# Two-layer hybrid diffusion step on one core: another order at the end of the expert stage and around the out-projection

## The chip, the cores and the metric

The kernel runs on one core of a Trainium2 chip. The metric is the device time of one execution in microseconds (us), as a median of several runs. Five engines work side by side, each through its own instructions in a fixed order: TensorE (PE, matrix products), VectorE (DVE), ScalarE (ACT), GpSimd (POOL) and SyncE (SP), which issues most of the transfers. An instruction that has to wait holds up everything behind it on its engine.

## What is computed

The reference runs two layers over 128 context tokens and 512 latent tokens of width 1024. Cut to what matters here:

```python
for l in range(DEPTH):                       # DEPTH = 2
    h = modulated(x)                         # scale and shift from the conditioning
    qa, ka, va, qb, kb, vb, qc, kc, vc, gc = split(h @ w_in)
    A = windowed attention(rope(qa), rope(ka), va, cached keys, sink)
    B = neighbourhood attention(qb, kb, vb, relative bias)
    C = swish(gc) * groupnorm(retention(qc, kc, vc, states))
    x = layernorm(alpha * x + gate * (concat(A, B, C) @ w_out))
    p = softmax(modulated(x) @ w_router)     # 16 experts, each takes its best tokens
    for e in range(16):                      # 64 latent and 16 context tokens each
        y[e] = (silu(xe @ w_gate) * (xe @ w_up)) @ w_down
    x = layernorm(alpha * x + gate * scatter(p * y))
```

All matrices are float32; the kernel splits each operand of a projection in a high part and a low part and multiplies three times (`mm3`: high by high, high by low, low by high).

## The kernel before

The 640 tokens are five tiles of 128: tiles 0 to 3 hold latent tokens, tile 4 the context. In each layer the work goes through four stages: the projections with the three head groups, the out-projection with the router, the experts, and the end of the experts with the second LayerNorm. Most of the order on the engines comes from a scheduler that works with the order in which the program is written, with `tc.issue_after(x)` (do not stand ahead of x) and with pools of buffers of limited size.

**Splitting.** `split` (L340 on) makes the high part on ACT (L344) and the low part on DVE or, with `E=G`, on GpSimd (L345). `weights(...)` does so for a chunk of weights of 1 MB: `wh` is the high part, `wl` the low part.

**Out-projection** (L1495 to L1545). For each tile `t`, `retention(u, cs)` (L1207 on) is started for the tiles `u` up to `t + 1`, one ahead. It makes scores (L1221), the products L1239 and L1243 into a PSUM buffer of the group "A", and then a chain of small instructions on one `work` buffer: the mean, L1252 (DVE), L1253 (ACT), L1255, L1256 and the root (DVE, then GpSimd L392), L1259, L1260 (DVE). After it PE transposes the result (L691, two matmuls) and a split puts it into `cs`, the operand of the tile's product. The product itself is L348 to L350, on PSUM buffers of group "A" too, in two halves of 512 columns with the weights `wo[0]`, `wo[1]` and then `wo[2]`, `wo[3]`; `wo[1]` and `wo[3]` are split on GpSimd (`WO = "0101"`). After the first half come L1373, L1374 (DVE), which write the residual tile `z`, the transposes L1387 and the logits L1395 of the router, which read a copy by ACT (L1391) or DVE (L1402).

**Experts** (L1873 to L1910). Per expert eight chunks `w_gate_up` (L1723, L1727) and four chunks `w_down` of 1 MB each go through 25 slots (`N_SLOTS`), loaded by SP. `down(e, aT)` (L1775) multiplies chunk by chunk: per chunk first the latent part (`lat`), then the context part (`cxt`). A slot comes free after its chunk.

**End of the experts.** Experts 0 to 13 are added to the token table in memory; the last two stay on chip. `on_chip` (L1810 on) weights the result of expert 14 (i = 0) and 15 (i = 1) and splits it: latent rows at L1819 and L1826, context rows at L1829, L1831, L1834. `begin` and `combine` (L1930, L1932) add them through one-hot matrices to the five tiles in PSUM. `ln2` (L1960 on) then walks a list, `OR1` between the layers and `OR2` after the last. Its steps are C (combine), L (statistics L610 to L616 and norm L1991), H (`turn_tile`: transposes L628, then the split into `hhi` and `hlo`, the operands of the next layer's projection), S (`store`: GpSimd L2011, L2014 over 128 x 1024, then the transfer to `xres`, L2015) and T (`tile_A`: the first projection of the next layer, keys and values of group A). `first_w` (L706) is the weight chunk of that first projection; its low part is made on DVE by four instructions of 128 x 512. `HG` (L117) says for which tile the half `kk = 0` of the `hlo` split is on GpSimd. After T4 follow the rotary step `rope` (L698 on: DVE L701, GpSimd L702, DVE L703 and L704) for the keys and then for each block of queries, and the chunks ci = 0, 1, ... of the next projection, each with a `wh` and a `wl`.

Of the kernel before, what the change touches and what calls it, by code (L numbers as in the profile page):

```python
# [63 lines left out]
OR1 = ["C0", "C1", "L0", "H0", "C2", "L1", "H1", "S0", "C3", "L2", "H2", "T0", "S1", "C4", "L3", "H3", "T1", "S2", "L4", "H4", "T2", "T3", "S3", "T4", "S4"]  # L64
OR2 = ["C0", "C1", "L0", "C2", "L1", "C3", "L2", "C4", "L3", "L4"]
# [12 lines left out]
NR = 1  # L78
# [32 lines left out]
NB = 0  # L111
# [4 lines left out]
SG = "0"  # L116
HG = "10000"  # L117
# [125 lines left out]
def hybrid_backbone_kernel(ctx: ExitStack, tc: tile.TileContext, a: dict):  # L243
# [94 lines left out]
    lo_op, hi_op = [], []  # L338

    def split(hi, lo, src, parts=1, E=V):  # L340
        w = src.shape[-1] // parts
        for i in range(parts):
            s = (Ellipsis, slice(w * i, w * i + w)) if parts > 1 else (Ellipsis,)
            hi_op[:] = [S.activation(hi[s], src[s], AF.Copy)]  # L344
            lo_op[:] = [E.tensor_tensor(lo[s], src[s], f32(hi[s]), op=ALU.subtract)]  # L345

# [362 lines left out]
    def start_A(l, w=None, first_in=False):  # L709
# [10 lines left out]
        ck = work()  # L720
        ld(ck[:, 0:128], a["cak"][l])
        split(kAh[:, 384:512], kAl[:, 384:512], ck[:, 0:128])
# [24 lines left out]
        return {"tab": tab, "kA": kA, "va": va}, tile_A  # L747

    def mixer(l, h, A, bg):
# [456 lines left out]

        def retention(t, cs):  # L1207
# [52 lines left out]
            V.tensor_mul(dd[:, 0:256], dd[:, 0:256], gC[:, 256 * t:256 * t + 256])  # L1260
# [227 lines left out]
        for t in range(NT):  # L1488
            ret = iter(())
            for u in range(t + 2):  # L1490
                if u == NT or u < NR or u in started:
                    continue
                started.add(u)
                if u < 4:
                    css[u] = sl.get(F32R, "cs")  # L1495
                ret = retention(u, css[u])
                if u == t:
                    drain(ret)
                else:
                    next(ret)  # L1500
# [36 lines left out]
        wo += [weights(AH_P, KP, E=G if WO[2 + i] == "1" else V) for i in range(2)]  # L1537
# [65 lines left out]
    def moe(l, gsel, idx, early, GB1, init, ctx_places, picked):  # L1603
# [171 lines left out]
        def down(e, aT):  # L1775
            last = e - (NE - 2)
            pl, pc = (psA(), psA()) if last == 1 else (psB(), psB())
            for k in range(4):
                ahead.fill(99, keep(e))
                w = ahead.next()  # L1780
                with in_turn("T"):
                    for i in range(2):
                        lat(pl, aT, w[:, 1024 * i:1024 * i + 1024], 2 * k + i)
                    for i, n in ((0, 0), (0, 1), (1, 0), (1, 1)):
                        cxt(pc, 2 * i + n, aT, w[:, 1024 * i + 512 * n:1024 * i + 512 * n + 512], 2 * k + i, k == 0, k == 3)
                sl.free(w)
# [22 lines left out]
        def on_chip(i, e, pl, pc, y):  # L1809
# [7 lines left out]
            for n in range(2):  # L1817
# [3 lines left out]
                with tc.issue_after((lo_op[0] if i and l + 1 < DEPTH else sq_last[0]).ins):  # L1821
# [6 lines left out]
            tC, yc = hf.get(F32, "yC"), hf.get(F32, "yc")  # L1828
            S.activation(tC[0:64, 0:512], pc[64:128], AF.Copy)  # L1829
            with tc.issue_after(lo.ins):  # L1830
                V.tensor_tensor(tC[0:64, 512:1024], pc[0:64], tC[0:64, 0:512], op=ALU.add)  # L1831
                for n in range(2):
                    r = slice(32 * n, 32 * n + 32)
                    V.scalar_tensor_tensor(yc[q, 512 * n:512 * n + 512], tC[r, 512:1024], gateC[r, e:e + 1],  # L1834
                                           g2[r, 512:1024], op0=ALU.mult, op1=ALU.mult)
                split(Ch[q], Cl[q], yc[q])
            hf.free(tC, yc)
# [75 lines left out]
        hf.free(aTs, last_aT, g2)  # L1913
# [38 lines left out]

        begin(0)
        begin(1)
        return combine, sums.ins

    def ln2(l, combine, sums):
# [44 lines left out]
        def store(t):  # L2002
# [6 lines left out]
            if SPN:  # L2009
                with tc.issue_after(pool_last[0]):  # L2010
# [7 lines left out]
        for f, t in [(o[0], int(o[1])) for o in (OR2 if h is None else OR1)]:  # L2018
            if f == "C":
                xs.append(combine(t))  # L2020
            elif f == "L":
                norm(t)
            elif f == "H":
# [171 lines left out]
```

## Time and profile before

| | us |
|---|---|
| median of 3 runs (lowest to highest) | 1911.55 (1911.55 to 1911.81) |
| the profiled execution | 1910.83 |
| its span on the trace | 1909.1 |
| PE busy | 1804.8 (95%) |
| DVE busy | 1137.1 (60%) |
| ACT busy | 423.9 (22%) |
| POOL busy | 242.0 (13%) |

The span goes from the first to the last instruction; 1.7 us of the profiled execution lie around it. Layer 0's out-projection lies at about 325 to 415 us of the span, its experts at 434 to 943, the boundary between the layers at 943 to 1020; layer 1's out-projection lies at about 1253 to 1344, its experts at 1365 to 1873, and the end of the last layer at 1873 to 1909. A busy share of 95% for PE says little about a place: what counts there is the gap ahead of an instruction on PE and the engine that ended it.

### The profile page before, as it was taken

What the parts mean: (1) busy time and instruction counts of PE and PEld (TensorE: products, weight loads), DVE (VectorE), ACT (ScalarE), POOL (GpSimd) and SP (SyncE); (2) the same over time, 40 slices, a digit from 0 to 9 for tenths busy, and PEclk for the clock granted to TensorE, in tenths of its full rate; (3) what the DMA queues carried; (4) which work ended last, traced back from release to release, by engine and by line L of the source; (5) the groups of instructions that cost most, each with busy time, mean ns of one, the idle gap of its engine ahead of it and who ended that gap; (6) DMA issues with size and microseconds to landing.
All of it is one profiled execution on the core that took longest, in us unless ns stands there. A gap on an engine that the chain in (4) does not pass through costs nothing.

```text
span 1909.1 us, 34582 instructions
## 1 busy us (share of the span) xinstructions
PE 1804.8 (95%) x14223; PEld 901.1 (47%) x14223; DVE 1137.1 (60%) x2968; ACT 423.9 (22%) x898; POOL 242.0 (13%) x188
## 2 busy tenths in 40 slices
PE   6999999899999999999879999998899999999995
PEld 3866777773333332222257767787533333222222
DVE  3654537566565655475586555574685757465657
ACT  2354533221000000000153655322200000000002
POOL 3200002221100000000061000121300000000003
PEclk9999999998999999999989999998899999999998
DMA  9333544289999999999933343325999999999994
GB/s 375 117 134 138 200 152 134 108 322 347 397 398 397 397 398 400 401 408 415 400 115 131 127 141 135 107 83 209 345 399 400 399 397 399 398 398 407 408 416 165
DMA packets 95886, 554.62 MB, mean 291 GB/s; under 512 B 13818, under 2 KB 18832, under 8 KB 36336
## 3 DMA queue, kind: packets, MB, share of 16 engines
q1 hardware_dynamic: 89776, 532.71, 70.7%
q0 software_dynamic: 5952, 19.69, 4.3%
q8 instruction: 112, 1.84, 0.4%
q14 instruction: 46, 0.38, 0.1%
HBM read 526.31 MB, written 26.05 MB: 289 GB/s over the span
## 4 chain that ended last, share of the span: by engine, by line
PE 56%; DMA 35%; DVE 5%; issue 2%; ACT 1%; POOL 0%; SPq 0%; DVEq 0%; ACTq 0%; POOLq 0%
DMA w<-wgu 22%; DMA w<-wdn 10%; PE pA L1723 10%; PE pA L348 7%; PE pA L349 6%; PE pA L350 6%; PE pA L1727 5%; PE pB L1723 3%; PE pB L356 2%; PE pC L813 2%; PE pB L1727 2%; PE pA L517 2%; PE pA L917 1%; PE pB L1395 1%; PE pA L1485 1%
## 5 line engine op out<-in xcount | busy, mean ns | idle before, releaser
L1723 PE MATMUL pA<-w,xT 128*32 128x512 f32 x4096 | 488.3, 597 | 12.0 <-DMA w<-wgu 9.3
L1723 PEld LDWEIGHTS pA<-w,xT 128*32 128x32 f32 x4096 | 130.0, 110 | 326.3 <-issue 275.7
L1727 PE MATMUL pA<-w,xT 128*32 128x512 f32 x2048 | 263.8, 592 | 0.0
L1723 PE MATMUL pB<-w,g 128*32 128x512 f32 x1920 | 229.8, 596 | 7.1 <-DMA w<-wdn 7.1
L1727 PEld LDWEIGHTS pA<-w,xT 128*32 128x32 f32 x2048 | 66.2, 110 | 153.6 <-issue 153.0
L1723 PEld LDWEIGHTS pB<-w,g 128*32 128x32 f32 x1920 | 61.2, 110 | 154.9 <-issue 122.4
L1727 PE MATMUL pB<-w,g 128*32 128x512 f32 x960 | 124.8, 592 | 0.0
L1642 DVE STREAM_TRANSPOSE g<-z 32x128 f32<-32x128 f32 x384 | 116.2, 303 | 6.4
L1642 DVE STREAM_TRANSPOSE catB<-xg 32x256 f32<-32x256 f32 x240 | 104.4, 435 | 4.0
L348 PE MATMUL pA<-hhi,wh 128*128 128x512 f32 x224 | 92.0, 411 | 0.0
L350 PE MATMUL pA<-hhi,wl 128*128 128x512 f32 x224 | 88.2, 396 | 0.6 <-DVE wl L328 0.6
L349 PE MATMUL pA<-hlo,wh 128*128 128x512 f32 x224 | 88.2, 394 | 0.0
L1805 POOL DMA_INDIRECT acc<-catB,idx x22 | 31.3, 1424 | 437.6 <-DVE catB L1801 437.6
L1765 ACT ACTIVATE z<-pA 128x512 f32<-128x512 f32 x18 | 10.7, 597 | 336.8 <-DVE xT L1659 165.6
L1642 DVE STREAM_TRANSPOSE g<-xg 32x128 f32<-32x128 f32 x240 | 72.6, 303 | 3.9
L345 DVE TENSOR_TENSOR wl<-w,wh 128x1024 fp32r<-128x1024 f32 (+2 forms) x46 | 54.5, 1220 | 33.4 <-ACT wh L344 13.9
L1623 POOL DMA_INDIRECT xg<-znd,idx x30 | 35.1, 1171 | 293.4 <-DVE catB L1642 238.6
L348 PE MATMUL pA<-wh,cs 128*128 128x512 f32 x160 | 68.0, 426 | 0.5 <-DVE gC L1140 0.3
L344 ACT ACTIVATE wh<-w 128x1024 fp32r<-128x1024 f32 (+2 forms) x50 | 53.7, 1119 | 61.9 <-DMA w<-win 25.0
L1727 PEld LDWEIGHTS pB<-w,g 128*32 128x32 f32 x960 | 31.1, 110 | 72.6 <-issue 72.6
L348 PE MATMUL pA<-wh,hhi 128*128 128x256 f32 x192 | 59.5, 313 | 5.7 <-ACT hhi L344 3.8
L350 PE MATMUL pA<-wh,cs 128*128 128x512 f32 x160 | 64.5, 405 | 0.0
(530 smaller groups left out, 2918.7 us busy)
## 6 DMA issues: line engine op xcount, KB each, us to landing
w<-wgu SPq DMA_DIRECT2D x256, 1024.0 KB, 21.5
w<-wdn SPq DMA_DIRECT2D x128, 1024.0 KB, 21.3
wada<-wada SPq DMA_DIRECT2D x48, 1024.0 KB, 4.9
w<-win SPq DMA_DIRECT2D x20, 1024.0 KB, 7.1
w<-wout SPq DMA_DIRECT2D x8, 1024.0 KB, 5.2
znd<-z SPq DMA_DIRECT2D x8, 512.0 KB, 5.7
acc<-z SPq DMA_DIRECT2D x8, 512.0 KB, 14.8
bias<-bias SPq DMA_DIRECT2D x8, 384.0 KB, 4.8
```

Source lines behind the costliest of these rows:

```text
L344: hi_op[:] = [S.activation(hi[s], src[s], AF.Copy)]
L345: lo_op[:] = [E.tensor_tensor(lo[s], src[s], f32(hi[s]), op=ALU.subtract)]
L348: T.matmul(out, lh, rh, start=first, stop=False)
L349: T.matmul(out, lh, rl, start=False, stop=False)
L350: return T.matmul(out, ll, rh, start=False, stop=last).ins
L356: T.matmul(out, (lh, ll)[x], (rh, rl)[y], start=first, stop=last)
L517: T.matmul(pm[32 * g:32 * g + 32, :], mst[:, k, :], w[:, 512 * g:512 * g + 512], start=(k == 0), stop=(k == 7))
L813: T.transpose(pt[:, 128 * b:128 * b + 128], s[:, o + 128 * b:o + 128 * b + 128], ident)
L1623: r = G.indirect_dma_start(out=xg[0:CAP, 0:1024], out_offset=None, in_=znd[l], in_offset=IndirectOffsetOnAxis(ap=idx[:, e:e + 1], axis=0))
L1642: sq_last[:] = [V.transpose(out, rows.rearrange("p (k q f) -> p k q f", q=4, f=32)[:, :, q, :])]
L1723: last_of["T"] = T.matmul(p[32 * g:32 * g + 32], x[:, 64 * ko + 32 * i:64 * ko + 32 * i + 32], w[:, 512 * n:512 * n + 512], start=(ko == 0 ...
L1727: last_of["T"] = T.matmul(p[32 * g:32 * g + 32], x[:, 512 + 32 * ko:544 + 32 * ko], w, start=first, stop=last).ins
```

## The change

1. `NR` goes from 1 to 2 and the loop of the out-projection runs to `t + 3`: retention is started two tiles ahead of the tile whose product is written. `wo[2]` is split on DVE in two parts, not ahead of the last retention's L1260; `wo[3]` is split on GpSimd as before.
2. In `OR1` the stores S0 to S4 move behind T2 and later, and are not to stand ahead of the last split on GpSimd (`g_op`).
3. The context part of expert 15 (`rest_`) becomes a step of its own, Y0, after tile 0's norm (both lists). The split of the cached keys becomes a step K0.
4. `down(15)` multiplies all four latent parts first, then the context parts, and holds its four slots until then. The latent part of `on_chip` for expert 15 stands behind expert 14's last split (`yk["end"]`).
5. `NB` = 1 keeps the statistics of the tiles in the order of the list. `SG` = "1" puts the low part of layer 1's `first_w` on GpSimd. `HG` = "11111" puts half of the `hlo` splits of every tile on GpSimd, where before that was tile 0's alone.

```diff
-OR1 = ["C0", "C1", "L0", "H0", "C2", "L1", "H1", "S0", "C3", "L2", "H2", "T0", "S1", "C4", "L3", "H3", "T1", "S2", "L4", "H4", "T2", "T3", "S3", "T4", "S4"]
-OR2 = ["C0", "C1", "L0", "C2", "L1", "C3", "L2", "C4", "L3", "L4"]
+OR1 = ["C0", "C1", "L0", "Y0", "H0", "C2", "L1", "H1", "K0", "C3", "L2", "H2", "T0", "C4", "L3", "H3", "T1", "L4", "H4", "T2", "T3", "S0", "S1", "T4", "S2", "S3", "S4"]
+OR2 = ["C0", "C1", "L0", "Y0", "C2", "L1", "C3", "L2", "C4", "L3", "L4"]
-NR = 1
+NR = 2
-NB = 0
+NB = 1
-SG = "0"
-HG = "10000"
+SG = "1"
+HG = "11111"
...
-            for u in range(t + 2):
-                if u == NT or u < NR or u in started:
+            for u in range(t + 3):
+                if u >= NT or u < NR or u in started:
...
-        wo += [weights(AH_P, KP, E=G if WO[2 + i] == "1" else V) for i in range(2)]
+        wo.append(weights(AH_P, KP, 2, after=r_last[0]))
+        wo.append(weights(AH_P, KP, E=G))
...
+                ws.append(ahead.next())
                 with in_turn("T"):
...
+                    lats(k)
+                    if last < 1:
+                        cxts(k)
+                if last < 1:
+                    sl.free(ws[k])
+            if last == 1:
+
+                with in_turn("T"):
+                    for k in range(4):
+                        cxts(k)
+                sl.free(*ws)
...
-                with tc.issue_after((lo_op[0] if i and l + 1 < DEPTH else sq_last[0]).ins):
+                with tc.issue_after(yk["end"] if i else sq_last[0].ins):
...
-                with tc.issue_after(pool_last[0]):
+                with tc.issue_after(g_op[0]):
                     G.tensor_tensor(y, x, gb[:, 0:1024], op=ALU.mult)
...
+            elif f == "Y":
+                rest_of_y(dve_last[0])
```

What this does to the order on three engines follows. In these rows a name with a number is one buffer (`cs_3116` one tile's operand, `wh` and `wl` the weights' parts, `work_86` the buffer of the retention's chain, `z_...` a residual tile). The line numbers of after are its own: L693 there is L691 before, L1398 is L1387, L1254 is L1243, L704 is L702, L706 is L704, L2054 and L2057 are L2011 and L2014.

On PE, in layer 0's out-projection, this stands between the transposes of two successive retention tiles before:

```order
L691 MATMUL pC<-cst,work_86 128x128 x2
L1239 MATMUL pA<-S_102_2672,m_101_2647 128x128 x2
L348 MATMUL pA<-wh_2957,cs_2961 128x512
L349 MATMUL pA<-wl_2958,cs_2961 128x512
L1387 MATMUL pC<-cst,z_2971 128x128 x4
L348 MATMUL pA<-wh_2951,cs_3116 128x512
L349 MATMUL pA<-wl_2952,cs_3116 128x512
L350 MATMUL pA<-wh_2951,cs_3116 128x512
```

and this now:

```order
L693 MATMUL pC<-cst,work_86 128x128 x2
L350 MATMUL pA<-wh_2995,cs_2947 128x512
L351 MATMUL pA<-wl_2996,cs_2947 128x512
L352 MATMUL pA<-wh_2995,cs_2947 128x512
L350 MATMUL pA<-wh_2995,cs_2947 128x512
L351 MATMUL pA<-wl_2996,cs_2947 128x512
L352 MATMUL pA<-wh_2995,cs_2947 128x512
L693 MATMUL pC<-cst,work_86 128x128 x2
L1398 MATMUL pC<-cst,z_3009 128x128 x4
```

Before, 22 matmuls of a product stand there after the router's transposes (the last three rows go on in the same way for the next tile) until the next two L691. Now six stand between two tiles' transposes, since retention tiles hold the PSUM buffers of group "A" that the next tile's product would need.

Also on PE, the place of the last retention tile (the context tile). It stands among the first products of a tile before:

```order
L1243 MATMUL pA<-vcxC_1865,work_86 128x64 x2
L1221 MATMUL pB<-vcxC_1865 128x128 x4
L1243 MATMUL pA<-vcxC_1865,work_86 128x64 x4
L691 MATMUL pC<-cst,work_86 128x128 x2
```

and now:

```order
L1406 MATMUL pB<-m_106_2894,work_85 128x16 x2
L1254 MATMUL pA<-vcxC_1865,work_86 128x64 x3
L1406 MATMUL pB<-m_106_2894,work_85 128x16 x2
L351 MATMUL pA<-wl_2996,cs_3071 128x512
L352 MATMUL pA<-wh_2995,cs_3071 128x512
L350 MATMUL pA<-wh_2995,cs_3071 128x512
L351 MATMUL pA<-wl_2996,cs_3071 128x512
L352 MATMUL pA<-wh_2995,cs_3071 128x512
L693 MATMUL pC<-cst,work_86 128x128 x2
```

Before, the transposes stand right behind the last L1243; now five matmuls of a product (`cs_3071`) and two of the router lie between.

On DVE, at the boundary between the layers, the key rope and the first weight splits of the next layer's projection stand like this before (`z` holds the keys, `wl_8001` is chunk ci = 1):

```order
L703 TENSOR_TENSOR work_7376<-work_7376,tab_7462 128x512
L328 TENSOR_TENSOR wl_7885<-w_7414,wh_7884 128x2048
L745 COPY xg_3280<-xg_3280 128x128
L704 TENSOR_TENSOR z_3126<-z_3126,work_7376 128x512
L345 TENSOR_TENSOR wl_8001<-w_7428,wh_8000 128x1024 x2
```

and the split for ci = 1 stands here now (`wl_8004`, after the ropes of the keys and of two blocks of queries, `qA`):

```order
L705 TENSOR_TENSOR work_7378<-work_7378,tab_7454 128x512
L345 TENSOR_TENSOR cxq_7882<-pC,cxq_7882 128x256
L706 TENSOR_TENSOR work_7378<-work_7378 128x512
L345 TENSOR_TENSOR qA_7880<-work_7378,qA_7880 128x2x128
L345 TENSOR_TENSOR wl_8004<-w_8001,wh_8003 128x1024 x2
```

The split for ci = 1 has moved behind the second block's L706, which needs that block's instruction on GpSimd.

On GpSimd at the same place, the last stores and the ropes before:

```order
L2011 TENSOR_TENSOR xg_3279<-xg_3279,ln_339_7474 128x1024
L2014 TENSOR_TENSOR xg_3279<-xg_3279,ln_339_7474 128x1024
L702 TENSOR_TENSOR z_3126<-z_3126,tab_7462 128x512
L702 TENSOR_TENSOR work_7376<-work_7376,tab_7462 128x512 x4
```

and now:

```order
L345 TENSOR_TENSOR hcx_7463<-work_7378,hcx_7463 128x512
L2054 TENSOR_TENSOR xg_3279<-xg_3280,ln_337_7464 128x1024
L2057 TENSOR_TENSOR xg_3279<-xg_3279,ln_337_7464 128x1024
L2054 TENSOR_TENSOR xg_3280<-catB_1836,ln_337_7464 128x1024
L704 TENSOR_TENSOR z_3162<-z_3162,tab_7454 128x512
L2057 TENSOR_TENSOR xg_3280<-xg_3280,ln_337_7464 128x1024
L2054 TENSOR_TENSOR z_3162<-catB_1836,ln_337_7464 128x1024
L704 TENSOR_TENSOR work_7378<-work_7378,tab_7454 128x512
L2054 TENSOR_TENSOR xg_3279<-z_3162,ln_337_7464 128x1024
L2057 TENSOR_TENSOR z_3162<-z_3162,ln_337_7464 128x1024
L2054 TENSOR_TENSOR xg_3280<-xg_3279,ln_337_7464 128x1024
L704 TENSOR_TENSOR work_7378<-work_7378,tab_7454 128x512
```

All ten instructions of the stores stood ahead of the ropes; now they stand between them.

## Rows read from the trace of the kernel before

**Rows 1.** Page, part 2: PE and DMA in 40 slices.

```profile
PE   6999999899999999999879999998899999999995
...
DMA  9333544289999999999933343325999999999994
```

**Rows 2.** Page, part 4: the chain that ended last, by engine.

```profile
PE 56%; DMA 35%; DVE 5%; issue 2%; ACT 1%; POOL 0%; SPq 0%; DVEq 0%; ACTq 0%; POOLq 0%
```

**Rows 3.** PE's waits, 300 to 415: waited for; total, times, longest.

```profile
PE pC L691 <- DVE work L1260: 3.5, 1, 3.5
PE pC L1387 <- DVE z L1374: 1.6, 1, 1.6
PE pA L1243 <- DVE work L1225: 0.8, 1, 0.8
```

**Rows 4.** Windows around 367: PE's busy time and clock behind the longest stall.

```profile
367.00:372.00 5.00, 5.00 (x21) 4.40 (x22) 2.98 (x8) 1.32 (x3) 1.01 (x1) 0.57 0.41 174
```

**Rows 5.** Timeline of the retention chain (DVE, POOL): start, duration, what.

```profile
367.63 0.42 DVE L1252 TENSOR_TENSOR work<-pA,mu 128x256 f32<-128x256 f32 x1 [0.78 <-PE pC L691]
...
369.57 1.01 POOL L392 TENSOR_TENSOR rs<-rsv,half 128x4 f32<-128x4 f32 x1 [3.64 <-DMA w<-wout]
...
371.66 0.41 DVE L1260 TENSOR_TENSOR work<-work,gC 128x256 f32<-128x256 f32 x1
```

**Rows 6.** Timeline of PE and ACT: a product's pace, `wo[3]`'s high part.

```profile
346.50 0.39 PE L349 MATMUL pA<-wl,cs 128*128 128x512 f32 x1
346.73 0.39 PE L350 MATMUL pA<-wh,cs 128*128 128x512 f32 x1
...
372.15 1.92 ACT L344 ACTIVATE wh<-w 128x2048 fp32r<-128x2048 f32 x1 [3.07 <-DVE work L1260]
```

**Rows 7.** Timeline: a GpSimd split, and DVE beside one.

```profile
325.54 4.58 POOL L345 TENSOR_TENSOR wl<-w,wh 128x2048 fp32r<-128x2048 f32 x1 [0.19 <-ACT wh L344]
...
325.55 4.58 DVE L1982 SCALAR_TENSOR_TENSOR GBT<-modT,lnT 128x2 f32<-128x2 f32 x1
```

**Rows 8.** PE's waits, 940 to 1080: waited for; total, times, longest.

```profile
PE pA L350 <- DVE hlo L345: 3.0, 3, 2.1
PE pC L628 <- ACT xg L1991: 2.5, 1, 2.5
```

**Rows 9.** Timeline of PE from the first to the last tile, then ci = 1.

```profile
965.99 1.32 PE L628 MATMUL pC<-cst,xg 128*128 128x128 f32 x8 [2.54 <-ACT xg L1991]
...
994.77 1.03 PE L628 MATMUL pC<-cst,xg 128*128 128x128 f32 x8
...
1019.83 0.39 PE L350 MATMUL pA<-hhi,wl 128*128 128x512 f32 x1
```

**Rows 10.** Timeline of GpSimd and DVE at the boundary.

```profile
979.20 2.85 POOL L2011 TENSOR_TENSOR xg<-catB,ln 128x1024 f32<-128x1024 f32 x1
...
1012.15 1.80 POOL L702 TENSOR_TENSOR work<-work,tab 128x512 f32<-128x512 f32 x1 [9.01 <-DVE work L701]
...
977.10 2.69 DVE L345 TENSOR_TENSOR hlo<-work,hhi 128x512 fp32r<-128x512 f32 x1
...
998.80 0.69 DVE L345 TENSOR_TENSOR hcx<-work,hcx 128x512 fp32r<-128x512 f32 x1 [0.32 <-ACT hcx L344]
...
1005.95 2.35 DVE L345 TENSOR_TENSOR wl<-w,wh 128x1024 fp32r<-128x1024 f32 x2
```

**Rows 11.** Timeline of DVE at the end of the last layer.

```profile
1873.02 1.53 DVE L1819 SCALAR_TENSOR_TENSOR z<-pA,gateL,g 64x512 f32<-64x512 f32 x2 [2.59 <-PE pA L1723]
...
1876.45 0.68 DVE L1831 TENSOR_TENSOR xg<-pA,xg 64x512 f32<-64x512 f32 x1
1877.17 1.49 DVE L1834 SCALAR_TENSOR_TENSOR z<-xg,gateC,g 32x512 f32<-32x512 f32 x2
...
1881.21 1.22 DVE L345 TENSOR_TENSOR yl<-z,yl 32x1024 fp32r<-32x1024 f32 x1
...
1901.05 2.34 DVE L1994 TENSOR_TENSOR xg<-xg,ln 128x512 f32<-128x512 f32 x2
```

More of the change, by code (lines that the diff above doesn't have):

```diff
@@ L336, in weights @@
         return hi, lo
-    lo_op, hi_op = [], []
+    lo_op, hi_op, g_op = [], [], []
     def split(hi, lo, src, parts=1, E=V):
@@ L719, in start_A, with cached @@
         tokk = va[:, 768:1024]
-        ck = work()
+        ck = work() if first_in else hf.get(F32, "ck")
         ld(ck[:, 0:128], a["cak"][l])
-        split(kAh[:, 384:512], kAl[:, 384:512], ck[:, 0:128])
+        def cached():
+            split(kAh[:, 384:512], kAl[:, 384:512], ck[:, 0:128])
+            if not first_in:
+                hf.free(ck)
+        if first_in:
+            cached()
         ld(vA[:, 3, :], a["cav"][l])
@@ L745, in tile_A @@
                 V.tensor_copy(va[:, 640:768], tokk[:, 128:256])
-        return {"tab": tab, "kA": kA, "va": va}, tile_A
+        return {"tab": tab, "kA": kA, "va": va, "cached": cached}, tile_A
     def mixer(l, h, A, bg):
@@ L1205, in states @@
             yield
+        r_last = []
         def retention(t, cs):
@@ L1777, in down, with lats, cxts @@
             pl, pc = (psA(), psA()) if last == 1 else (psB(), psB())
+            ws = []
+            def lats(k):
+                for i in range(2):
+                    lat(pl, aT, ws[k][:, 1024 * i:1024 * i + 1024], 2 * k + i)
+            def cxts(k):
+                for i, n in ((0, 0), (0, 1), (1, 0), (1, 1)):
+                    cxt(pc, 2 * i + n, aT, ws[k][:, 1024 * i + 512 * n:1024 * i + 512 * n + 512], 2 * k + i, k == 0, k == 3)
             for k in range(4):
                 ahead.fill(99, keep(e))
-                w = ahead.next()
+                ws.append(ahead.next())
                 with in_turn("T"):
[L1782 to L1786, printed above, removed]
+                    lats(k)
[8 more added lines that the diff above has]
+                sl.free(*ws)
             y = hf.get(F32, "y")
@@ L1827, in on_chip, with rest_ @@
             hf.free(y)
[L1828 to L1837, printed above, removed]
+            yk["end"] = lo.ins
+            def rest_():
+                tC, yc = hf.get(F32, "yC"), hf.get(F32, "yc")
+                S.activation(tC[0:64, 0:512], pc[64:128], AF.Copy)
+                with tc.issue_after(yk["end"]):
+                    V.tensor_tensor(tC[0:64, 512:1024], pc[0:64], tC[0:64, 0:512], op=ALU.add)
+                    for n in range(2):
+                        r = slice(32 * n, 32 * n + 32)
+                        V.scalar_tensor_tensor(yc[q, 512 * n:512 * n + 512], tC[r, 512:1024], gateC[r, e:e + 1],
+                                               g2[r, 512:1024], op0=ALU.mult, op1=ALU.mult)
+                    split(Ch[q], Cl[q], yc[q])
+                yk["end"] = lo_op[0].ins
+                hf.free(tC, yc)
+            if i:
+                yk["rest"] = rest_
+            else:
+                rest_()
         yk = {}
@@ L1951, in combine, with rest_of_y, ln2 @@
             return sums_of[t], accs[t]
+        def rest_of_y(after):
+            with tc.issue_after(after):
+                yk["rest"]()
+            hf.free(g2)
         begin(0)
         begin(1)
-        return combine, sums.ins
-    def ln2(l, combine, sums):
+        return combine, sums.ins, rest_of_y
+    def ln2(l, combine, sums, rest_of_y):
         h = GB = A = None
@@ L2022, in ln2 @@
                 norm(t)
+            elif f == "K":
+                with tc.issue_after(h_last[1][0]):
+                    A["cached"]()
+            elif f == "Y":
+                rest_of_y(dve_last[0])
             elif f == "H":
```

6 lines of the change are left out of this document (4 added, 2 removed).

## The prediction

> **What bounds the kernel now.** I read the slices first [rows 1]. PE is at nine tenths nearly everywhere, and where DMA is at nine tenths too (the two expert stages) the experts' weights pace the stage; the chain says the same in one line, 56% PE, 35% DMA, 5% DVE [rows 2]. A busy share of 95% cannot tell what an edit is worth, so I then read PE's own waits in the two places that the change touches. In layer 0's out-projection the list has one large entry, 3.5 us of PE waiting for L1260, the last instruction of a retention tile; 1.6 for the residual tile and 0.8 for a score follow [rows 3]. Layer 1's list names the same instructions. Behind the 3.5 us stall the granted clock is 0.57 over 5.0 us [rows 4], a mixture of the two levels of 1.2 and 2.4 GHz, after PE had done little. At the boundary the list says that PE waits for the low parts of `h`, 3.0 us, and for the normed tile, 2.5 us [rows 8]. From the first tile's transposes (965.99) to the last tile's (994.77) pass 28.8 us, or 7.2 a tile, and the point from which PE has work without a gap is the first chunk after the key projection, ci = 1, at 1019.83 [rows 9].
>
> A delay or a gain at the end of the out-projection goes on to the end of the expert stage nearly one to one: SP's expert loads stand behind the stores of the residual tiles, which that end makes. So I count it at full size, and come to the opposite case among the rivals.
>
> **Retention two tiles ahead.** What it removes in a layer: the three stalls, 3.5 + 1.6 + 0.8 = 5.9, and the half clock, 5.0 x (1 - 0.57) = 2.1; together 8.0 us [rows 3, 4]. The count of new stalls comes from the order on PE and the length of the chain. From L1252's start to L1260's end pass 372.07 - 367.63 = 4.4 us, 1.0 of it on GpSimd [rows 5]; about 0.7 of these lie behind a DVE instruction of the product, so I take 3.8, and 0.5 for the mean ahead of it. The chain needs `work_86`, so the next tile's chain starts only when PE has transposed this one. A matmul of the product costs 0.23 us [rows 6].
>
> - Between the transposes of tiles 1 and 2 stand six matmuls, 1.4 us, where 22 stood: the stall is 3.8 + 0.5 - 1.4 = 2.9.
> - Between tiles 2 and 3 stand six and the router's work, so 0.4 to 1.8; I take 1.1.
> - Behind the context tile's products stand two logits and five matmuls, 1.5 us. Here DVE has the residual tile's instructions in between, so that I put the chain at 6.1 and the stall at 4.6.
> - The high part of `wo[3]` (1.92 on ACT [rows 6]) stands ahead of the copies that the router's logits read. Some 0.9 of it lies beside matmuls; 1.0 is left.
> - The first product of tile 2 waits for the residual tile, 0.7, by less than today's 1.6 [rows 3].
> - At the start two tiles go through the chain before the first product is over: 0.9 to 1.6, I take 1.2.
>
> The sum is 2.9 + 1.1 + 4.6 + 1.0 + 0.7 + 1.2 = 11.5 against 8.0, so **+3.5 us a layer**. The reason for it is not the length of the chain but the order: two retention tiles ahead take the PSUM buffers of group "A", and the next tile's 18 matmuls, the cover of the chain, come after them. Low end: DVE lets the chain through everywhere (each stall 0.5 to 1.5 shorter), 7 to 8 us of stalls, so -1. High end: a GpSimd split of `wo[1]` falls into the chain. What that costs is seen once: a small DVE instruction, begun 0.01 us after GpSimd's split of 4.58 us, took 4.58 itself [rows 7]. Retention's DVE instructions with both inputs in SBUF (L1260 and the splits of `cs`) would be held in the same way; part of it is in the 1.2 above, so +3.5 more, to +7. Two layers: **+7, from -2 to +14**.
>
> **The end of the experts between the layers.** Expert 15's context part (L1831, L1834 and its split, 0.68 + 1.49 + 1.22 = 3.4 us on DVE by the same instructions of the last layer [rows 11]) leaves the way to tile 0's statistics, and with it the context half of the last weight chunk on PE, about 1.2 (half of 509 us over 192 chunks). So tile 0's transposes come 4.6 earlier, at about 961.4. The GpSimd splits of `first_w` stand at the start of this and hold DVE for a time, but what they hold is waiting for expert 15 anyway; I cost them at nothing, and up to 2 if they last into expert 14's last split. The tiles then go faster: the stores are off GpSimd. Beside a store a low split took 2.69, alone 0.69 [rows 10]. The 3.0 us for which PE waits for such splits [rows 8] go. So PE would stand before ci = 1 at 1019.83 - 4.6 - 3.0 = 1012.2, near 1012.8 with some loss.
>
> Here the stores return. Ten of them at 2.36 to 2.85 [rows 10] start on GpSimd at about 990.4 (last tile's transposes 987.4 plus its split). Up to the second block's rope there stand, by the order, eight stores and three ropes of 1.80 [rows 10]: 8 x 2.45 + 3 x 1.8 = 25.0, so 1015.4 at the earliest, 1016 to 1019 with the waits of the ropes for DVE. On DVE the low split of ci = 1 stands behind that rope's last step now, where it stood ahead of the query ropes. It adds 0.7 + 0.4 and 2.35 in two halves [rows 10]: `wl` is there at 1019.5 to 1022, while PE is ready at 1012.8. PE meets a stall of 7 to 9 us just where today it arrives at 1019.83. So the gain of 7 is taken back: **0, from -6 to +4**. The low end is the case in which the ropes get through between the stores; the high end has DVE's ropes and splits held by stores.
>
> The row on the held split [rows 10] has a rule of the Trainium skill beside it ("SBUF — State Buffer", "Who interferes with whom"): GpSimd's SBUF ports are DVE's second pair, and a DVE instruction with both inputs in SBUF contends with a GpSimd instruction that reads SBUF. The trace agrees, 2.69 beside a store and 0.69 without [rows 10], 4.58 beside a split [rows 7]. The rule speaks against moving splits from DVE to GpSimd: by it the four splits of `first_w` and each store between the ropes would hold DVE, and the boundary would stand at its high end, +4, and the whole at 1923.5.
>
> **The end of the last layer.** DVE runs from L1819 at 1873.02 almost without a gap to L1994's end at 1903.39 [rows 11] and is what ends the kernel. The context part (3.4) only moves behind tile 0's norm; DVE's sum of work is the same. The latent products gain about 0.9 at the start. The statistics in list order take away the freedom to use a tile that is early. I put it at **+1, from -1 to +3**.
>
> **The sum.** 1910.83 (the profiled execution; the median is 0.7 above it) + 7 + 0 + 1 = 1918.8, or 1919.5 on the scale of the median.
>
> **Rivals.**
> - *The stores do not hold ci = 1* (faster). Price: the 7 us of the boundary stay. Condition: GpSimd has done the second block's rope before PE is ready, 1012.8; the count above says 1016 to 1019, so it needs the stores to start 3 to 6 us earlier, or the scheduler's gate to let PE use the time for the ropes' scores. Against it: eight stores are counted in the order. With the out-projection at +1 rather than +7 it gives about 1906. If also the old stalls (8.0 a layer) go and half of the new ones do not come, 8.0 - 5.8 = 2.2 a layer are gained and the time is about 1901.
> - *New stalls smaller, gains cancel* (no change). The out-projection's low end (-2 to +2) and the boundary at 0: about 1911. For it: my chain of 6.1 for the context tile rests on DVE instructions that may give way.
> - *The expert stage hides the out-projection's delay* (no change, about 1912 to 1913). The loads run at nine tenths through the stage [rows 1], and if they start as early as now, PE catches up on loaded chunks. Against: two of the first loads apart, they stand behind the residual stores on SP.
> - *PE gets tile 0 still earlier*: if expert 14's part is not held by ACT's high parts of `first_w`, transposes at 954 rather than 961.4. The stores then start earlier by as much and the first rival's condition is met. It is part of the first rival's chance.
>
> **How the numbers follow.** Slower as summed, with the boundary at -1 to +4 and the out-projection at +3 to +12: 1915 to 1928, chance 0.5. Cases without a change of size (the second and third rival): 0.2. Faster (first and last rival): 1895 to 1907, chance 0.3; a boundary of +4 on top of a no-change case adds a little to slower. About 0.2% is what a measurement can tell here (3.8 us, 1907.7 to 1915.4). That makes faster 0.28, same 0.20, slower 0.52. The likeliest case's own range is 1915 to 1928. The range reaches down until about 0.1 is left below, 1902, and up to 1928 with 0.1 above.
>
> **What would show it.** In the profile of the changed kernel PE's list at the out-projection should lose the wait for L1260's place at 3.5 and show several of 1 to 5 us for the same instruction (two or three transposes, the context tile's the longest). The expert stage should begin 2 to 5 us later in each layer. At the boundary tile 0's transposes should come 4 to 5 us earlier after the experts' end, the `hlo` waits should be gone, and PE should wait 5 to 9 us for a low split at ci = 1, with DVE waiting for GpSimd's rope ahead of it. If PE's list has no entry over 2 us at either place, the forecast is wrong and the faster case holds. If the out-projection ends where it does today, its matmuls found a cover that I did not see.

## The result, and the profile after

| | before | after |
|---|---|---|
| median (lowest to highest), us | 1911.55 (1907.63 to 1911.81) | 1938.91 (1935.51 to 1941.2) |
| span of the profiled execution | 1909.1 | 1938.1 |
| mean granted clock | 0.977 | 0.966 |

The ratio is 1.0143, with a 95% interval of 1.0127 to 1.0159. The change makes the kernel slower by 27 us; forecast was 1919.5, in a range of 1902 to 1928. The sign was right, the size was not, and the time lies outside the range.

To see where the 29.0 us of span went, cut both traces at the same five points and split each stretch three ways from the windows view: the time in which PE had nothing running (idle), the busy time times one minus the granted clock (clock loss), and the rest (work).

| stretch | before | after | difference | idle | clock loss |
|---|---|---|---|---|---|
| start to the first state product of retention, layer 0 | 302.2 | 301.6 | -0.7 | | |
| to the first expert matmul, layer 0 (out-projection) | 132.4 | 150.4 | **+18.0** | 14.5 to 19.7 | 5.3 to 16.3 |
| to the first one-hot matmul (experts) | 520.6 | 518.9 | -1.7 | 14.9 to 12.8 | 3.8 to 4.0 |
| to the state products of layer 1 (boundary, projections) | 276.1 | 286.5 | **+10.4** | 13.0 to 21.6 | 3.9 to 7.7 |
| to the first expert matmul, layer 1 (out-projection) | 133.8 | 136.6 | +2.8 | 13.8 to 15.4 | 7.3 to 9.6 |
| to the end | 544.0 | 544.1 | +0.1 | 29.7 to 28.9 | 2.3 to 2.9 |

PE's waits of the kernel after in layer 0's out-projection, 330 to 390 (engine, line waited for: total, times, longest), against [rows 3]:

```profile
PE pC L693 <- DVE work L1271: 7.5, 2, 4.7
PE pA L1254 <- DVE work L1236: 1.4, 1, 1.4
PE pB L1406 <- ACT work L1402: 1.1, 1, 1.1
PE pA L350 <- DVE work L1384: 0.8, 1, 0.8
PE pA L1250 <- DVE work L1263: 0.5, 1, 0.5
PE pA L350 <- ACT cs L344: 0.5, 1, 0.5
```

L693 and L1271 are L691 and L1260 of before. The one stall of 3.5 us has become two, 2.87 and 4.67, with smaller ones around them: 11.8 us in all. What stands behind the stalls shows in the windows of the same kernel (window, its length, PE busy, PEld, DVE, ACT, POOL, granted clock, DMA share, GB/s):

```profile
354.00:364.00 10.00, 6.66 (x28) 5.07 (x27) 5.85 (x15) 2.12 (x5) 1.11 (x2) 0.82 0.00 0
364.00:374.00 10.00, 10.00 (x35) 8.31 (x34) 4.10 (x9) 0.98 (x2) 0.91 (x1) 0.50 0.17 53
374.00:384.00 10.00, 5.73 (x32) 4.61 (x31) 4.09 (x12) 0.42 (x1) 1.01 (x1) 1.00 0.41 156
384.00:394.00 10.00, 8.46 (x26) 6.87 (x27) 3.12 (x5) 2.67 (x3) 4.59 (x1) 0.51 0.48 171
```

From 364 to 374 PE never waits and runs at 0.50, the lower level of 1.2 GHz throughout: 35 matmuls in 10 us. Before, the clock of these 10 us is 0.66, with 5.0 us at 0.57 behind the one stall [rows 4]:

```profile
364.00:374.00 10.00, 7.09 (x29) 6.13 (x30) 6.06 (x17) 3.16 (x4) 2.01 (x2) 0.66 0.49 203
```

The wait of 1.4 in the list (L1254, at 338.13) has a cause of its own. The split of `wo[1]` on GpSimd falls into the retention of two tiles, and a DVE instruction with both inputs in SBUF takes 4.52 us beside it, where it took 0.68 before:

```profile
332.62 4.57 POOL L345 TENSOR_TENSOR wl<-w,wh 128x2048 fp32r<-128x2048 f32 x1 [4.28 <-ACT wh L344]
333.22 4.52 DVE L1241 TENSOR_TENSOR m<-qkC,m 128x512 f32<-128x512 f32 x1
```

Around that wait and behind it the clock is 0.79 over 334 to 344 and 0.86 over 344 to 354, where it was 1.00 before.

In layer 1 the list is shorter: 6.2 in two waits for L1271 (the longest 3.4), 1.1 for L1402 and 0.5 for a split of `cs`, 7.8 us in all.

At the boundary tile 0's transposes come 7.5 us behind the one-hot matmul (978.42 and 970.90), 10.8 before. The first matmul that needs the new `wl` stands 44.6 us behind it (1015.52), 50.2 before (1005.35): a gain of 5.5. The gain stands up to the first matmul of ci = 1, 58.8 us behind the one-hot matmul (64.2 before). Then the waits of PE, 1025 to 1050:

```profile
PE pA L352 <- DVE wl L345: 8.6, 1, 8.6
PE pB L358 <- ACT qA L344: 1.8, 1, 1.8
PE pB L358 <- DVE qA L345: 1.4, 1, 1.4
```

And GpSimd and DVE ahead of that wait, on the timeline of the kernel after (start, duration, what):

```profile
1008.12 2.40 POOL L2054 TENSOR_TENSOR xg<-xg,ln 128x1024 f32<-128x1024 f32 x1
...
1027.40 1.77 POOL L704 TENSOR_TENSOR work<-work,tab 128x512 f32<-128x512 f32 x1
1029.13 2.39 POOL L2054 TENSOR_TENSOR xg<-z,ln 128x1024 f32<-128x1024 f32 x1
1031.47 2.80 POOL L2057 TENSOR_TENSOR z<-z,ln 128x1024 f32<-128x1024 f32 x1
1034.24 2.53 POOL L2054 TENSOR_TENSOR xg<-xg,ln 128x1024 f32<-128x1024 f32 x1
1036.74 1.44 POOL L704 TENSOR_TENSOR work<-work,tab 128x512 f32<-128x512 f32 x1
...
1029.20 2.86 DVE L706 TENSOR_TENSOR work<-work 128x512 f32<-128x512 f32 x1 [1.19 <-POOL work L704]
1032.62 4.44 DVE L345 TENSOR_TENSOR qA<-work,qA 128x256 fp32r<-128x256 f32 x2
1038.98 2.49 DVE L706 TENSOR_TENSOR work<-work 128x512 f32<-128x512 f32 x1
1041.96 2.00 DVE L345 TENSOR_TENSOR qA<-work,qA 128x256 fp32r<-128x256 f32 x1 [0.48 <-ACT qA L344]
1043.88 2.35 DVE L345 TENSOR_TENSOR wl<-w,wh 128x1024 fp32r<-128x1024 f32 x2
```

Before, the same rope step (L704 there) and the pair of `qA` splits take this:

```profile
1018.89 0.69 DVE L704 TENSOR_TENSOR work<-work 128x512 f32<-128x512 f32 x1 [1.16 <-POOL work L702]
1020.07 0.76 DVE L345 TENSOR_TENSOR qA<-work,qA 128x256 fp32r<-128x256 f32 x2 [0.49 <-ACT qA L344]
```

Now they take 2.5 to 2.9 and 4.44: the first L706 and the pair end within 0.6 us behind the end of a store instruction on GpSimd (1029.13 + 2.39 = 1031.5 for the first L706, which ends at 1032.1; 1034.24 + 2.53 = 1036.8 for the pair, which ends at 1037.1). Three of the ten store instructions run ahead of the first rope, five between it and the third, two behind, so eight stand ahead of the second block's rope, as the prediction counted. GpSimd's queue and the held DVE together bring the first half of `wl` of ci = 1 to about 1045, 74 us behind the one-hot matmul.

### The profile page after: what moved, and what is told of

Same layout as the page of the kernel before. It is cut to its first block, busy times and chain, and to the rows that moved or that the text cites. A ratio compares the mean times of both kernels' runs of the same rounds, so it can differ in the third digit from the quotient of the medians.

```text
span 1938.1 us, 34582 instructions
## 1 busy us (share of the span) xinstructions
PE 1821.0 (94%) x14223; PEld 914.0 (47%) x14223; DVE 1138.3 (59%) x2962; ACT 424.9 (22%) x900; POOL 256.4 (13%) x196
## 4 chain that ended last, share of the span: by engine, by line
DMA 50%; PE 40%; DVE 5%; issue 2%; ACT 1%; POOL 1%; SPq 0%; DVEq 0%; ACTq 0%; POOLq 0%
DMA w<-wgu 29%; DMA w<-wdn 16%; PE pA L350 7%; PE pA L352 6%; PE pA L351 6%; PE pA L1736 3%; PE pB L358 2%; PE pC L822 2%; DMA acc<-z 2%; PE pA L519 1%; PE pA L926 1%; PE pB L1406 1%; DMA w<-win 1%; PE pA L1496 1%; PE pB L493 1%
## 5 line engine op out<-in xcount | busy, mean ns | idle before, releaser
L1778 ACT ACTIVATE z<-pA 128x512 f32<-128x512 f32 x18 | 10.8, 597 | 334.6 <-DVE xT L1672 184.5
L350 PE MATMUL pA<-wh,cs 128*128 128x512 f32 x160 | 70.2, 440 | 1.7 <-ACT cs L344 0.9
L352 PE MATMUL pA<-wh,cs 128*128 128x512 f32 x160 | 67.1, 420 | 0.0
L351 PE MATMUL pA<-wl,cs 128*128 128x512 f32 x160 | 67.1, 419 | 0.0
```

Of the source, the lines that this page charges most:

```text
L350: T.matmul(out, lh, rh, start=first, stop=False)
L351: T.matmul(out, lh, rl, start=False, stop=False)
L352: return T.matmul(out, ll, rh, start=False, stop=last).ins
```

## The experiments

Times are medians, ratios are to the kernel before on the same chip, with their 95% interval. Runs on different chips are compared here by their medians; the kernel before's own median differs by up to 2 us between the chips (1909.57 to 1911.55), and where the ratios give another difference, both are said. Stretches and clock losses are those of one profiled execution of each kernel. The runs fall in five groups.

### Which edit loses what: undoing

`e1_ret_back` puts retention one tile ahead again in the changed kernel:

```diff
-NR = 2
+NR = 1
-            for u in range(t + 3):
-                if u >= NT or u < NR or u in started:
+            for u in range(t + 2):
+                if u == NT or u < NR or u in started:
```

> The changed kernel with retention one tile ahead again (NR = 1, t + 2), all else as changed. The trace of the changed kernel puts 17.4 us of its loss in layer 0's out-projection and 2.8 us in layer 1's. If the retention order is the cause: 1917 to 1921 us, the end of layer 0's out-projection 15 to 18 us earlier. If the new places of the last two weight splits or the later loads are the cause: above 1930 us.

Measured: 1930.17 us, 1.0107 (1.0089 to 1.0126), 7 (by the ratios) to 9 us less than the kernel after, at the edge of the second expectation and not in the first. Layer 0's out-projection goes from 150.4 to 140.6, layer 1's from 136.6 to 129.9. That leaves 8 us over 132.4 in layer 0, so retention is not all of it.

`e2_stores_back` puts S0 to S4 back between the tiles, with the old gate `pool_last[0]`:

> The changed kernel with the five stores at their old places in the list between the layers, all else as changed. The trace puts 10.4 us at the boundary, a gain of 5.5 up to the first chunk and a loss of 16 behind it. If the stores beside the rotary steps are the cause of the loss: 1922 to 1929 us, and no wait of PE over 2 us for the low part of ci = 1. If the GpSimd splits of the first weight chunk are the cause: 1935 us or more.

Measured: 1926.04 us, 1.0075 (1.0054 to 1.0096). The stretch at the boundary falls from 286.5 to 274.2, and its idle time from 21.6 to 10.3. The first theory holds.

`e3_both_back` undoes both:

> The changed kernel with both taken back: retention one tile ahead and the stores at their old places. If the two losses add: 1902 to 1909 us, faster than the kernel before by what latent products first and the GpSimd splits give. If the rest of the change is worth nothing by itself: 1910 to 1914 us.

Measured: 1917.45 us, 1.0034 (1.0021 to 1.0046): outside both expectations, still slower than before. Layer 0's out-projection stands at 141.6 with retention as it was. The new split of `wo[2]` is an edit that was left there. `e10_three_back` takes it back as well:

```diff
-        wo.append(weights(AH_P, KP, 2, after=r_last[0]))
-        wo.append(weights(AH_P, KP, E=G))
+        wo += [weights(AH_P, KP, E=G if WO[2 + i] == "1" else V) for i in range(2)]
```

> The changed kernel with retention, the split of wo[2] and the stores taken back; what is left is the latent products first, the context part later, the statistics in order and the splits on GpSimd. If these bring tile 0 forward and it stays: 1903 to 1908 us. If the gain at the boundary is taken back there: 1909 to 1913 us.

Measured: 1906.76 us, 0.9979 (0.9969 to 0.9989): **faster than before** by 4 us. What is left of the change (latent products first, the later context part, the statistics in order and the splits on GpSimd) is worth that together; the three edits taken back lost it and 27 us more. Layer 0's out-projection is back at 132.4.

### Each alone on the kernel before

> The kernel before with retention two tiles ahead (NR = 2, t + 3) and nothing else. Taking this back from the changed kernel gave 8.7 us. If the order alone costs it: 1918 to 1927 us, with waits of 3 to 5 us ahead of the transposes of retention tiles 2 and 4 and a clock below full behind them. If it costs only together with the new split of wo[2]: 1909 to 1914 us.

`e4_ret_alone` (the first diff, turned round): 1929.55 us, 1.0099 (1.008 to 1.0117). Its two main entries are those of the kernel after:

```profile
PE pC L691 <- DVE work L1260: 7.5, 2, 4.7
PE pB L1395 <- ACT work L1391: 1.1, 1, 1.1
```

So the order alone costs, 18.5 us, a little above the expected range.

> The kernel before with the new split of wo[2] alone (in two parts, not ahead of the last retention's L1260). With retention and stores taken back the changed kernel still had 9 us more in layer 0's out-projection. If this split is the cause: 1916 to 1921 us. If not: 1909 to 1913 us.

`e11_wo_alone` (the second diff, turned round): 1922.62 us, 1.0059 (1.0042 to 1.0075). A split of a weight chunk in two parts, behind L1260, costs 11.5 us. The two do not add: both together, with the rest as in `e10`, are `e2`, 19.3 us over `e10`.

> The kernel before with the five stores at the end of the list between the layers and nothing else (S0 and S1 behind T3, S2 to S4 behind T4). If the stores beside the rotary steps cost by themselves: 1916 to 1923 us. If the place is only bad together with the GpSimd splits of the changed kernel: 1908 to 1913 us.

`e6_late_alone`: 1911.29 us, 1.0 (0.9991 to 1.001). The late stores alone cost nothing. With the old gate the first began at 977.04, between the tiles, as GpSimd had little else to do.

> The kernel of e10_three_back with the stores at the changed kernel's late places, but with the old gate (not ahead of the last root on GpSimd, instead of the last GpSimd split). If the new gate is what pushes the ten store instructions into the rotary steps: 1904 to 1911 us, and the first store 10 us earlier than in the changed kernel. If the late places do it together with the GpSimd splits: 1915 to 1921 us.

> The kernel of e10_three_back with the changed kernel's late stores and its gate (not ahead of the last GpSimd split). e16_gate with the late stores and the old gate took 1911.3 us. If the gate carries the boundary's loss: 1915 to 1920 us, first store at about 50 us behind the experts' end, PE waiting over 5 us for a low part at ci = 1. If the loss needed the other edits too: 1909 to 1913 us.

On `e10`, which has the splits on GpSimd, the late places cost 4.5 us with the old gate (`e16_gate`: 1911.31 us, 1.0002, 0.9991 to 1.0013) and 10 us, by the ratios 12, with the new one (`e14_late_gate`: 1916.95 us, 1.0042, 1.0027 to 1.0056). The first store stands 9.5 us behind the one-hot matmul in `e10`, 27.6 in `e16`, 37.2 in `e14` and in the kernel after. `e14` also has the 8.6 us wait at ci = 1, `e16` one of 1.4. (For `e14` the first store was expected at about 50 us.) Of the loss of `e14` the gate carries somewhat more than half.

### Is the half clock a price of its own?

`e5_busy` puts matmuls that compute nothing into PE's two longest stalls:

```diff
+            pt = psC()
+            if t in (2, 4):
+                with tc.issue_after(sq_r.ins):
+                    for _ in range(12 if t == 2 else 20):
+                        T.matmul(pt[:, 0:256], ident, cst[:, 0:256], start=True, stop=True)
```

> The changed kernel with 12 and 20 matmuls that compute nothing put into PE's two longest stalls of each out-projection (ahead of the transposes of retention tiles 2 and 4, into a buffer that the transposes then overwrite). Nothing waits for less. If most of layer 0's loss is the half clock behind those stalls (16.7 us of clock loss there against 5.1 before): 1926 to 1934 us and a granted clock near 1.0 behind them. If the loss is the waiting itself: 1937 to 1941 us.

Measured: 1938.34 us, 1.015 (1.0121 to 1.018), no gain, but with single runs at 1933 to 1934 and at 1942. In the profiled one (span 1932.7) layer 0's clock loss falls from 16.3 to 5.8, and the filler is much longer than the stalls, two passes of 0.22 us for each matmul: PE's work in that stretch rises by 13.1 us. `e17_fill` has 6 and 9 in place of 12 and 20:

> As e5_busy, with the filler cut to the stalls: there 12 and 20 matmuls took two passes of 0.22 us each, 5.3 and 8.8 us for stalls of 2.9 and 4.7 us; here 6 and 9, some 2.6 and 4.0 us. If the half clock behind the stalls is a price of its own in the changed kernel: 1926 to 1934 us, layer 0's out-projection 6 to 11 us shorter with its clock loss under 8 us (16.3 before). If the waiting alone costs: 1936 to 1941 us.

Measured: 1922.99 us, 1.0077 (1.0062 to 1.0093), 16 us less than the kernel after by the medians and 13 by the ratios. Layer 0's out-projection is 137.7 instead of 150.4 and layer 1's 130.0 instead of 136.6. The clock loss falls from 16.3 to 7.1 and from 9.6 to 3.7, which is 15 of these 19 us. The rest is not the clock: the filler changed PE's order too. Between the context tile's last L1254 and its transposes stand six matmuls of a product, eight of the router's logits, router transposes and the filler now, where five matmuls of a product and four logits stood, so some waits are filled with work that has to be done anyway (idle time and work together fall by 3.5 us in layer 0 and by 0.8 in layer 1). The same windows as above in `e17_fill`:

```profile
354.00:364.00 10.00, 10.00 (x55) 8.45 (x53) 5.30 (x15) 2.20 (x5) 1.01 (x1) 1.00 0.00 0
364.00:374.00 10.00, 9.96 (x52) 8.12 (x51) 5.79 (x16) 1.40 (x3) 2.20 (x2) 1.00 0.54 202
374.00:384.00 10.00, 9.21 (x54) 7.79 (x54) 8.51 (x10) 3.50 (x4) 4.76 (x2) 1.00 0.42 140
384.00:394.00 10.00, 10.00 (x55) 8.49 (x54) 4.19 (x11) 1.73 (x2) 0.55 (x1) 1.00 0.63 240
```

From 354 on the clock stands at 1.00, against 0.82, 0.50, 1.00 and 0.51. That is the main term that the forecast had at nothing.

The same on the good kernel, `e10`, whose longest stall is the 3.5 us of [rows 3]:

> The kernel of e10_three_back (1906.8 us) with 12 matmuls that compute nothing in each layer's longest stall, ahead of the transposes of retention tile 3. Nothing waits for less. If half clock behind a stall is a price of its own (2.1 us behind the 3.5 us stall in the kernel before): 1902.5 to 1905.5 us, granted clock 1.0 behind it. If the clock is not moved by what PE does in the stall: 1906 to 1910 us.

> The kernel of e10_three_back with 6 matmuls (2.6 us) in the 3.5 us stall ahead of the transposes of retention tile 3, where e15_busy had 12 that ran 7.1 us. If a filled stall keeps the clock: 1902 to 1906 us. If the clock falls for what lies ahead of the stall too, or the filler delays the transposes: 1906 to 1911 us.

Both lost: 1918.66 us, 1.0046 (1.0032 to 1.006), with 12 matmuls that ran 7.13 us (`e15_busy`), and 1925.23 us, 1.0085 (1.0072 to 1.0098), with 6 (`e18_fill3`). In this order the filler starts behind waits of 0.80 and 0.55 us, and the clock falls all the same: it is 0.72 over 361 to 367 in both (0.76 in `e10`), and the passes of `e18` take 0.38 us each, not 0.22 (4.54 us for 12). Over 367 to 373 it is 1.00 in both, where `e10` has 0.67. So the filler brings the clock back sooner and does not keep it. What makes the 18 us of `e18` is something else, which the next section shows. The 12 us of `e15` are not explained: the instruction that is held in `e18` (L1391) takes 0.68 in it.

### GpSimd's hold on DVE beside the out-projection

DVE in `e18_fill3` at the place where `wo[3]` is split (start, duration, what), and GpSimd:

```profile
373.59 0.69 DVE L1390 TENSOR_TENSOR work<-pA,catB 128x512 f32<-128x512 f32 x1 [1.69 <-PE pA L352]
374.32 4.71 DVE L1391 SCALAR_TENSOR_TENSOR z<-z,work 128x512 f32<-128x512 f32 x1
378.95 0.41 DVE L345 TENSOR_TENSOR cs<-pC,cs 128x256 fp32r<-128x256 f32 x1
...
373.98 4.50 POOL L345 TENSOR_TENSOR wl<-w,wh 128x2048 fp32r<-128x2048 f32 x1 [2.99 <-ACT wh L344]
```

L1390, with one input in PSUM, takes 0.69. L1391, with both in SBUF, takes 4.71 and ends at 379.0, 0.55 us behind GpSimd's split (378.48). `e11_wo_alone` shows the same:

```profile
370.49 2.35 DVE L345 TENSOR_TENSOR wl<-w,wh 128x1024 fp32r<-128x1024 f32 x2
372.77 0.17 DVE L1404 COPY m<-pB 128x16 f32<-128x16 f32 x1
372.85 4.93 DVE L1376 SCALAR_TENSOR_TENSOR z<-z,work 128x512 f32<-128x512 f32 x1
...
372.65 4.59 POOL L345 TENSOR_TENSOR wl<-w,wh 128x2048 fp32r<-128x2048 f32 x1 [3.57 <-ACT wh L344]
...
377.89 1.09 PE L1389 MATMUL pC<-cst,z 128*128 128x128 f32 x4 [3.36 <-issue]
```

The copy from PSUM (L1404), begun 0.12 us behind GpSimd's split, takes 0.17; L1376, begun 0.20 behind it, takes 4.93. The new split of `wo[2]` (2.35 us) stands ahead of L1376, so L1376 starts 0.2 us after GpSimd's split of `wo[3]` rather than ahead of it, and PE meets a second stall of 3.36 us (the view puts it down to "issue"; L1389 reads `z` and starts 0.11 us behind the end of L1376). Layer 0's out-projection is 9.2 us longer than before, 3.4 of it idle and 4.4 clock loss. In the kernel before the same two met the other way round: L1374 was done when GpSimd began.

```profile
372.14 0.68 DVE L1374 SCALAR_TENSOR_TENSOR z<-z,work 128x512 f32<-128x512 f32 x1
374.15 4.57 POOL L345 TENSOR_TENSOR wl<-w,wh 128x2048 fp32r<-128x2048 f32 x1 [3.57 <-ACT wh L344]
```

`e20_wo_dve` is `e11` with the split of `wo[3]` on DVE, behind L1376:

```diff
-        wo.append(weights(AH_P, KP, E=G))
+        wo.append(weights(AH_P, KP))
```

> The kernel of e11_wo_alone (1922.6 us: the kernel before with the new split of wo[2]) with wo[3] split on DVE instead of GpSimd, behind the residual tile's instruction L1376. In e11 that instruction took 4.93 us instead of 0.69 while GpSimd split wo[3], and PE waited 3.4 us for it. If GpSimd's hold on DVE is the price of the new split: 1909 to 1914 us, L1376 at 0.69. If DVE's own queue is: 1918 us or more.

Measured: 1906.07 us, 0.9983 (0.9975 to 0.9992). 16.5 us (14.5 by the ratios) are gone with one word, and it is faster than before, which neither expectation had. The stall of 3.36 us is gone, and each layer's out-projection is 7.4 us shorter than in `e11`.

```profile
373.09 0.68 DVE L1376 SCALAR_TENSOR_TENSOR z<-z,work 128x512 f32<-128x512 f32 x1
373.69 2.28 DVE L345 TENSOR_TENSOR wl<-w,wh 128x2048 fp32r<-128x2048 f32 x1
```

> The kernel of e18_fill3 (1925.2 us: e10 with the longest stall filled) with wo[3] split on DVE behind the residual tile's L1391, which took 4.71 us there beside the GpSimd split. If that hold was what e18 lost: 1902 to 1908 us. If the filler itself costs: 1915 us or more.

`e19_fill_dve`: 1910.77 us, 1.0011 (0.9997 to 1.0026), between the two expectations. The hold was 14 of the 18 us that `e18` lost; its L1393 takes 0.69. The other 4 are left for the filler itself (3 against `e21`, which has no filler); single runs go from 1908 to 1923.

> The kernel of e10_three_back with wo[3] split on DVE and no filler, the control for the two above. If the split on GpSimd holds nobody in that kernel: 1905 to 1909 us, as e10. If it holds DVE there too: 1900 to 1904 us.

`e21_dve`: 1908.03 us, 0.999 (0.9982 to 0.9999), not told from `e10`: there the split on GpSimd holds nobody.

### Two that asked for more

> The kernel of e10_three_back without the ten store instructions on GpSimd at the boundary: the normed tiles go to memory as they are, and gain and bias of the norm are applied to the residual tiles when the next layer's out-projection loads them. If GpSimd's hold on DVE at the boundary is what still costs there: 1898 to 1904 us. If the same instructions cost as much beside the out-projection's retention: 1906 to 1915 us.

`e12_rz` (`RZ = 1` on `e10`; the transfers that are left of the stores stand at the late places of the list): 1913.89 us, 1.002 (1.001 to 1.0031). The boundary is 268.5 instead of 274.6, but the ten instructions stand beside layer 1's retention now, and that stretch goes from 133.4 to 144.6. There L1270 and L1271 take 2.57 and 2.44 us beside them, 0.42 alone, and PE's waits for L1271 grow to 9.0 in three.

> The kernel of e10_three_back with the splits moved to GpSimd taken back too (the first weight chunk and four of the five low parts on DVE again). What is left of the change is the latent products first, the context part later and the statistics in order. If the GpSimd splits carry the gain of 4 us: 1909 to 1912 us. If the order of expert 15 carries it: 1904 to 1908 us.

`e13_hgsg` (`SG = "0"`, `HG = "10000"` on `e10`): 1909.57 us, 0.9999 (0.9987 to 1.001), with single runs from 1905 to 1916. The medians say that the GpSimd splits bring 3 us, but the intervals of the two touch, and the boundary's stretch is 274.8 against 274.6. What of `e10`'s gain they carry stays open.

## Why the prediction was wrong, step by step

- **New stalls of the out-projection: the main ones right, the sum in part by luck.** Forecast for a layer were 2.9, 1.1, 4.6, 1.0, 0.7 and 1.2, together 11.5; layer 0's trace has 2.87, 4.67, 1.15, 0.78, 0.52, 0.47 and 1.38, together 11.8. That the six matmuls left between two transposes are the cover that is gone shows in the 2.87, and it is the same in `e4`. But the 1.1 between tiles 2 and 3 did not come (no wait there), and the 1.38 is a wait for a score, of the kind that was to go (0.8 [rows 3]): it stands behind L1241, which took 4.52 beside the split of `wo[1]`. That is the prediction's high end, on another instruction than it named. In layer 1 the stalls are 7.8, not 11.5.
- **The half clock: this term failed, the largest miss.** The sum counted the half clock that goes (2.1 us a layer [rows 4]) and none that comes behind the new stalls. Measured is a clock loss of 16.3 instead of 5.3 us in layer 0 (+11.0) and 9.6 instead of 7.3 in layer 1 (+2.3). So the out-projections cost 18.0 + 2.8 = 20.8, not 7. `e17_fill` bears it out: with the stalls filled the clock loss falls by 15 us in the two layers. Some 3 of layer 0's 11 lie at 334 to 354, behind the wait of 1.38, which layer 1 does not have. Why the same stalls cost so differently is not shown: `e4` has the 7.5 us of two waits in both layers, and its clock loss is 10.8 (+5.5) in layer 0 and 9.8 (+2.5) in layer 1.
- **The split of `wo[2]` was not costed at all.** It stood in the forecast only as wo[3]'s `wh` on ACT (1.0). Alone it is worth 11.5 us, by the hold on L1374 (`e11`, `e20`). In the kernel after there is no such hold: its L1385 takes 0.68 and is done at 381.4, and GpSimd's split begins at 386.33. Whether the split costs anything there in another way was not tested by itself.
- **The boundary: the mechanism was right, its size was not.** Forecast was a gain of 7 up to ci = 1 and a stall of 7 to 9 that eats it. Measured are 5.5 gained, then 1.8 + 1.4 + 8.6 = 11.8 us of waits, and 3.8 of clock loss: +10.4 in the stretch, not 0. Two steps were too small. GpSimd's last rope ahead of the split ended 67.3 us behind the one-hot matmul; the forecast of 1016 to 1019 is 61 to 64. And the DVE instructions between that rope and the split were taken at their own times (0.7 + 0.4), where they took 2.49 and 2.00 beside the stores. The held DVE instructions are what the prediction had at its high end, +4. The Trainium skill's rule ("SBUF — State Buffer", "Who interferes with whom") says that a DVE instruction with two SBUF inputs contends with a GpSimd instruction that reads SBUF; the trace agrees, 0.69 became 2.86 and 0.76 became 4.44. The step at fault is that the hold was taken as an upper end, when [rows 7] and [rows 10] already showed such holds.
- **The end of the last layer:** forecast +1, measured +0.1 over the whole last stretch.
- **The delay goes on nearly one to one: right.** Layer 0's experts began 17.4 us later and ended 15.7 later; the stage took 518.9 for 520.6.
- **The rivals.** None of them came: no gain cancelled and the expert stage hid nothing. The forecast and all rivals shared the missing clock term, and so did the range. The sign was right because the stalls and the late `wl` came as forecast; the time was missed by the two sizes above, 13.8 us in the out-projections and 10.4 at the boundary.

The best times measured are `e20` (1906.07) and `e10` (1906.76). They change different places, and were not tried together.

## What to carry to other kernels

A stall on TensorE has to be priced twice: its own length, and the half clock behind it. Against the kernel before, idle time and clock loss rose by 5.2 and 11.0 us in layer 0 of the kernel after, by 1.6 and 2.3 in layer 1, and by 5.5 and 5.5, 2.8 and 2.5 in `e4`: about as much again, once twice as much. Where a change makes new stalls, that term belongs to the sum, as it does for the stalls that go. And before a GpSimd instruction of several us is placed, list the DVE instructions with both inputs in SBUF that may start while it runs, and who waits for them: in `e11` one of them started 0.2 us behind the GpSimd split and took 4.93 us, and moving that split off GpSimd was worth some 15 us.

## What the hardware showed that was not expected

- Filling a gap with matmuls that compute nothing made the kernel after 13 to 16 us faster (`e17_fill`), most of it since the clock stayed at 1.00. Filling a gap behind 1.3 us of waiting did not keep the clock: passes of 0.38 us, clock 0.76 over 361 to 367 in `e19_fill_dve`.
- A copy on DVE from SBUF to SBUF is held too: L754, 128x128, took 2.20 us beside a store (1015.59 in the kernel after), and 0.22 before.
- GpSimd seems to be held in its turn: its store at 1013.28 in the kernel after took 4.43 us, not 2.4, and it began while a DVE split (L328, 1011.00 to 1015.47) ran. This is one row and was not tested.
- Which of the two starts first can be turned by a moved split of 2.35 us: in `e11` L1376 started 0.2 us behind GpSimd's split, in the kernel before L1374 was done 1.3 us ahead of it.
